# An encoder layer on one core: the operand builder adds before it splits, and the embedding tiles move to other steps and another engine

## Chip, cores and metric

One core of one Trainium2 chip. The metric is the device time of one execution in microseconds (us), the median of several runs; less is better. The engines are named as in the profile: PE (TensorE, the matmuls), DVE (VectorE), ACT (ScalarE), POOL (GpSimd) and SP (SyncE, which only issues transfers). A DMA is a transfer.

## What is computed

One layer of a bidirectional encoder, 512 tokens of width 1024, all in fp32:

```
h = h + 0.5 * swiglu(rms_norm(h, g_ffn1), w_ffn1_gate, w_ffn1_up, w_ffn1_down)      # hidden width 2816
u = rms_norm(h, g_mix) @ w_in
h = h + concat([mla(u), diff_attention(u)]) @ w_out                                 # 8 + 4 heads
h = h + 0.5 * swiglu(rms_norm(h, g_ffn2), w_ffn2_gate, w_ffn2_up, w_ffn2_down)
gate = sigmoid(rms_norm(h, g_ple_in) @ w_ple_gate + b_ple_gate)
h = h + gate * rms_norm(p @ w_ple_proj, g_ple_out)
```

## The kernel before

**Numbers in two parts.** An fp32 operand is split into a high part (a cast to `fp32r` by ACT) and a low part (what the cast left out, a subtraction on DVE). Each product is then three matmuls (`mm3`: high by high, high by low, low by high; L409 to L411). Weights come as 512 KB chunks by DMA, are split the same way (`Chunk`: cast L124, low part L97) and feed PE.

**The two feed-forward layers.** Each runs its 22 hidden blocks in four groups: one *plain* group of 4 blocks (gate and up projections, then the down projection to eight output tiles m = 0 to 7, named `ps_d`), then three groups of 6 blocks in which each pair of blocks takes two calls of `seven`. `seven` computes a 2 by 2 block product with seven smaller products in place of eight (Strassen-Winograd). In the order of the code these are S2 by T2, A11 by B11, S1 by N1, S3 by N3, A12 by B21, S4 by B22 and A22 by N4; three banks r1, r2, r3 hold them, ACT and DVE move them out to `q1`, `q2`, `q3` (L573 to L597). The weight side of a call is a `Unit`: two chunks `ra`, `rb` and a half chunk `rc`, sums formed partly by accumulating DMAs on POOL's queue (L157, L158) and partly by two POOL additions (L174, L175), then split into the tiles xa, xb, xc, xs. ACT casts xs in two halves (L187, L193).

**The builder.** The activation side is made once in each layer by `Forms.build`, for two halves (kp = 0, 1). It scales four tiles of h into a buffer y, splits the pieces used as they are (`sa`), forms four combinations n1, t2, n3, n4 on DVE, and splits these (`put`: a cast and a subtraction on a page named `fm`). It is a generator: `build(n)` runs n steps of it between other work of the plain group. Two of its splits, n3 and n4 of each half, are not done in it but put on the list `rest`; `finish_one`, called four times in the first `seven`, does one of them each time. The buffer y comes from a pool of three (`hlq`) that the units' tiles xa, xb, xs use too; y is free when the last of the four combinations has been read out of it.

**Order.** In the feed-forward layers PE, DVE, ACT and POOL run in the order of the code, each as a queue of its own: an instruction that waits holds up everything behind it on its engine. `slot(us)` and `steps(n)` decide where the splits of the next chunks stand, and `held` counts buffers. In the attention stage between the layers only PE keeps the order of the code; the other engines' order is chosen by a scheduler when the program is built.

**The embedding tiles.** `p @ w_ple_proj` is made in the attention stage by `embed`: after a first step that loads p, eight steps of six matmuls each into one bank (`ps_pe`), copied out by ACT (L1000) and sent to DRAM by POOL's queue (L1001). The attention stage runs over steps s_; in step s_ one block of scores of one head is computed, earlier heads' probabilities are transposed and multiplied, and `FILL_STEPS[s_]` says which other work ("T", "K", "E") is put in. "E" is one step of `embed`.

Of the kernel before, what the change touches and what calls it, by code (L numbers as in the profile page):

```python
# [18 lines left out]
TT = S // P  # L19
# [16 lines left out]

FILL_PRE = "TTTTTTTTTTTTTKTKTKTTT"
FILL_MID = "TKK"
FILL_STEPS = ("T", "TTE", "TT", "TT", "T", "") + ("E", "") * 6 + ("",) * 15 + ("E", "E")
HEADS = "DDMDMDMMMMMM"  # L40

GC = {"ffn1": 0, "mix": 8, "ffn2": 16, "ple_in": 24, "ple_out": 32, "b_ple": 40,
# [7 lines left out]
def encoder_layer(ctx, tc, xT, pT, wst, gcols, rows, consts, out):  # L50
    nc = tc.nc
# [368 lines left out]
    n1 = Norm("ffn1", nc.vector)  # L420
# [71 lines left out]
    class Forms:  # L492
# [11 lines left out]
        def build(self, kp):  # L504
            def v(t):
                return t.rearrange("p (a b) -> p a b", b=HS)

            def put(i, src):
                pg_ = page(f"fm{i}")
                d = pg_.rearrange("p x (a b) -> p x a b", b=HS)  # L510
                split(d[:, 0], d[:, 1], src)
                self.pg[kp][i] = pg_

            held[1] += 1
            y = hl_tile(1, "y", F32)
            ks = (2 * kp, 2 * kp + 1, 2 * kp + 4, 2 * kp + 5)
            for i, k in enumerate(ks):
                nc.vector.scalar_tensor_tensor(out=y[:, i // 2, (i % 2) * S:(i % 2 + 1) * S], in0=h[k],
                                               scalar=g(self.name, k), in1=self.rbc, op0=ALU.mult, op1=ALU.mult)
                yield  # L520
            q = [y[:, i].rearrange("p (a b) -> p a b", b=S) for i in range(2)]
            b11, b12 = q[0][:, :, :HS], q[0][:, :, HS:]
            b21, b22 = q[1][:, :, :HS], q[1][:, :, HS:]
            for i, k in enumerate(ks):

                c = slice(0, HS if i < 2 else S)
                a = self.sa[k] = page(f"sa{k}")
                split(a[:, 0, c], a[:, 1, c], y[:, i // 2, i % 2 * S:i % 2 * S + c.stop])
                yield
            n1, t2_, n3, n4 = [v(t2(f"f{i}")) for i in range(4)]  # L530
            nc.vector.tensor_sub(n1, b11, b12)
            put(self.N1, n1)
            yield
            nc.vector.tensor_add(t2_, b22, n1)
            put(self.T2, t2_)
            yield
            nc.vector.tensor_sub(n3, b12, b22)
            nc.vector.tensor_sub(n4, b21, t2_)
            held[1] -= 1
            self.rest.insert(kp, lambda: put(self.N3, n3))  # L540
            self.rest.append(lambda: put(self.N4, n4))
            yield

# [13 lines left out]
    def seven(forms, after=None):  # L557

        F_ = Forms
        A11, A12, S1, A22, S3, S2, S4 = nxt()  # L560
        r1, r2, r3 = psum("r1"), psum("r2"), psum("r3")
        q1, q2, q3 = t2("q1"), t2("q2"), t2("q3")
        lo, hi = slice(0, HS), slice(HS, S)

        def mul(r, left, i, start):
            x, c0 = left
            for k in range(4):
                c = slice(c0 + k * P, c0 + (k + 1) * P)
                bh, bl = forms.at(i, k)
                mm3(r[:, lo], x[:, 0, c], x[:, 1, c], bh, bl, start and k == 0, k == 3, skip_group_check=True)  # L570

        mul(r2, S2, F_.T2, True)
        nc.scalar.copy(q2[:, hi], r2[:, lo])  # L573
        forms.finish_one()
        steps(1)
        mul(r1, A11, F_.B11, True)
        nc.scalar.copy(q1[:, lo], r1[:, lo])
        forms.finish_one()
        steps(2)
        mul(r3, S1, F_.N1, True)  # L580
        nc.vector.tensor_add(q2[:, lo], r3[:, lo], q1[:, lo])
        forms.finish_one()
        steps(2)
        mul(r2, S3, F_.N3, False)
        nc.vector.tensor_sub(q3[:, hi], r2[:, lo], q2[:, lo])  # L585
        nc.vector.tensor_sub(q1[:, hi], q1[:, lo], q2[:, hi])
        forms.finish_one()
        steps(1)
        mul(r1, A12, F_.B21, False)
        after(0, r1[:, lo])  # L590
        steps(1)
        mul(r3, S4, F_.B22, False)
        nc.vector.tensor_add(q2[:, hi], r3[:, lo], q1[:, hi])
        after(1, q2[:, hi])
        steps(2)
        mul(r2, A22, F_.N4, False)
        nc.vector.tensor_sub(q3[:, lo], r2[:, lo], q1[:, lo])  # L597
        after(2, q3)
        steps(2)

    def ffn(norm, after, side=None, early=None):
# [39 lines left out]
        forms = builder = None  # L641
# [6 lines left out]
        for gi, (f0, n, plain) in enumerate(FGROUPS):  # L648
            hts = []
            if plain:  # L650
                late = []
                for f in range(n):
                    if f == 0 and early is not None:
                        psg, psu = early
                    else:
                        psg = psum("ps_g")
                        proj(psg, nxt(), norm.act)
                        slot(5.4)
                        if f == 1:
                            st_["r4"] = col_rsqrt(norm.acc, DM)  # L660
                        build(1)
                        psu = psum("ps_u")
                        proj(psu, nxt(), norm.act)
                        slot(3.5, f < n - 1)
                    late.append((psg, psu, hts))
                    if f == 1:
                        st_["rbc"] = row_bcast(st_["r4"])
                        forms = Forms(norm.name, st_["rbc"])
                        builder = (x for kp in range(2) for x in forms.build(kp))
                    if f > 0:  # L670
                        for e in late:
                            evac(*e)
                        late = []
                        build(3)
            else:
                build(99)
                for f in range(0, n, 2):
                    pair(hts)
            heads = []
            if plain:  # L680

                w = nxt()
                for m in range(3):
                    if m == 2:
                        while not ready:
                            advance()
                        w = ready[0].out
                    heads.append(psum("ps_d"))
                    proj(heads[m], w, hts, m % 2 * n, range(n - 1))
                    slot(1.3)  # L690
                    build(1)
                w = used[0].out
            for m in range(KT):
                if not plain:
                    ps = psum("ps_d")
                    proj(ps, nxt(), hts)
                else:
                    if m % 2 == 0 and m > 0:
                        w = nxt()
                    if m < 3:  # L700
                        ps = heads[m]
                        proj(ps, w, hts, m % 2 * n, range(n - 1, n))
                    else:
                        ps = psum("ps_d")
                        proj(ps, w, hts, m % 2 * n)
                if gi < len(FGROUPS) - 1 or m < KT - 1:
                    slot(0.0 if plain and m < 2 else 0.68 * n - (2.2 if gi == len(FGROUPS) - 1 else 0.75))
                if plain:
                    d = t2("hd")
                    nc.scalar.activation(d, ps, AF.Copy, scale=0.5)  # L710
                    nc.gpsimd.dma_start(out=h[m], in_=d, accum_op=ALU.add)
                else:
                    nc.vector.scalar_tensor_tensor(out=h[m], in0=ps, scalar=0.5, in1=h[m],
                                                   op0=ALU.mult, op1=ALU.add)
                last = gi == len(FGROUPS) - 1
                if last:
                    after(m)
                elif side is not None and (gi == 1 and m < KT // 2 + 1 or gi == 2 and m == 3):
                    for _ in range(2):
                        next(side, None)  # L720
                build(1 if m < 2 else 2)

    nmix = Norm("mix")
    h_dram = drp.tile([KT, P, S], F32, name="h_dram")
# [256 lines left out]
    def embed():  # L981
# [8 lines left out]
        for m in range(KT):  # L990
            if m % 4 == 0:
                w = chunk()
            ps = psum("ps_pe")
            for k in range(2):
                c = slice(((m % 4) * 2 + k) * P, ((m % 4) * 2 + k + 1) * P)
                mm3(ps, w[:, 0, c], w[:, 1, c], pa[k][0], pa[k][1], k == 0, k == 1)
            if m % 2 == 0:
                pg_ = page("pe", dt=F32)
            pe = pg_[:, m % 2, :]
            nc.scalar.copy(pe, ps)  # L1000
            nc.gpsimd.dma_start(out=pe_dram[m], in_=pe)  # L1001
            yield

# [425 lines left out]
```

## Time and profile before

| | us |
|---|---|
| median of 3 runs | 1046.29 (1044.59 to 1047.51) |
| the profiled execution, whole | 1045.17 |
| its span, first to last instruction | 1043.4 |
| PE busy (share of the span) | 1016.5 (97%) |
| DVE busy | 746.5 (72%) |
| ACT busy | 532.8 (51%) |
| POOL busy | 321.0 (31%) |
| PE share of the chain that ended last | 84% |

The first feed-forward layer stands at about 0 to 380 us, with its first `seven` at 78 us; attention and its projections to about 640 us; the second feed-forward layer after it, its first `seven` at 703 us; the last gate ends the program. In a timeline row the first number is the start in us from the span's start, the second the duration; in square brackets stands how long the engine had been idle before it and what ended that. The granted clock is a share of full speed (1.00 is 2.4 GHz, a half is 1.2 GHz).

### The profile page before, as it was taken

To read this page: it belongs to the slowest core of one execution; us is meant where nothing else is said; L and a number is where in the kernel's file an instruction comes from. 1 tells how busy PE (TensorE), PEld (TensorE's weight loads), DVE (VectorE), ACT (ScalarE), POOL (GpSimd) and SP (SyncE) were. 2 spreads that over 40 slices of the span, in tenths; PEclk is the share of its full clock that TensorE was granted. 3 is DMA by queue.
4 is the path that set the end of the run, shared out by engine and by line. 5 is a ranking of instruction groups with operands and counts; after the bars stand their busy time and mean duration, and the time that the engine had idled before them with its cause. 6 is when DMAs were issued, how large, how long until landed. Compare 5 with 4: busy or idle time off the path is not lost.

```text
span 1043.4 us, 16021 instructions
## 1 busy us (share of the span) xinstructions
PE 1016.5 (97%) x6076; PEld 893.1 (86%) x6076; DVE 746.5 (72%) x1258; ACT 532.8 (51%) x914; POOL 321.0 (31%) x291
## 2 busy tenths in 40 slices
PE   9988999999999999999999999988999999999998
PEld 7868998998999898876767888868998998999887
DVE  7786864875587648788788764686866875587764
ACT  7445532552354557478787643455534552354531
POOL 1144412532251210026553312044416532252000
PEclk9999999999999999999999999999999999999999
DMA  6367655656564542222103022367656655566331
GB/s 243 119 167 179 157 158 132 165 140 181 124 172 109 156 165 90 91 78 79 52 1 122 21 91 92 90 168 178 160 172 192 169 136 178 122 175 193 112 101 60
DMA packets 52621, 137.94 MB, mean 132 GB/s; under 512 B 6112, under 2 KB 7008, under 8 KB 52544
## 3 DMA queue, kind: packets, MB, share of 16 engines
q1 hardware_dynamic: 36864, 106.88, 30.9%
q0 software_dynamic: 14096, 27.66, 14.9%
q10 hardware_dynamic: 1584, 2.39, 0.6%
q8 instruction: 47, 0.77, 0.3%
q14 instruction: 30, 0.25, 0.1%
HBM read 126.02 MB, written 6.29 MB: 127 GB/s over the span
## 4 chain that ended last, share of the span: by engine, by line
PE 84%; DVE 9%; DMA 2%; issue 2%; ACT 2%; POOL 0%; SPq 0%; ACTq 0%; DVEq 0%; POOLq 0%
PE r L411 11%; PE r L410 11%; PE r L409 11%; PE ps_d L409 6%; PE ps_d L410 6%; PE ps_d L411 6%; PE ps_in L409 2%; PE ps_in L410 2%; PE ps_in L411 2%; PE ps_pt L1179 2%; PE ps_pg L409 1%; PE ps_pg L411 1%; PE ps_pg L410 1%; PE ps_wo L409 1%; PE ps_wo L411 1%
## 5 line engine op out<-in xcount | busy, mean ns | idle before, releaser
L97 DVE TENSOR_TENSOR hl<-raw,hl 128x1024 fp32r<-128x1024 f32 (+4 forms) x110 | 118.4, 1089 | 67.4 <-ACT hl L124 65.9
L124 ACT CAST hl<-raw 128x1024 fp32r<-128x1024 f32 (+2 forms) x104 | 96.3, 943 | 104.4 <-DMA raw<-in_wst_dram 30.5
L411 PE MATMUL ps_d<-ht,hl 128*128 128x512 f32 x352 | 137.3, 390 | 1.9 <-DVE hl L97 1.9
L409 PE MATMUL ps_d<-ht,hl 128*128 128x512 f32 x352 | 137.3, 390 | 0.0
L410 PE MATMUL ps_d<-ht,hl 128*128 128x512 f32 x352 | 137.1, 389 | 0.0
L174 POOL TENSOR_TENSOR ra<-ra,rb 128x512 f32<-128x512 f32 x36 | 49.6, 1378 | 219.2 <-DVE xa L97 214.3
L409 PE MATMUL r<-fm,xb 128*128 128x256 f32 x288 | 81.9, 284 | 4.5 <-DVE q L585 4.5
L409 PE MATMUL r<-sa,xa 128*128 128x256 f32 x288 | 82.3, 286 | 0.0
L410 PE MATMUL r<-sa,xa 128*128 128x256 f32 x288 | 82.3, 286 | 0.0
L411 PE MATMUL r<-sa,xa 128*128 128x256 f32 x288 | 82.2, 285 | 0.0
L410 PE MATMUL r<-fm,xb 128*128 128x256 f32 x288 | 81.6, 283 | 0.0
L411 PE MATMUL r<-fm,xb 128*128 128x256 f32 x288 | 81.5, 283 | 0.0
L411 PEld LDWEIGHTS ps_d<-ht,hl 128*128 128x128 f32 x352 | 66.1, 188 | 16.5 <-DVE hl L97 2.8
L409 PEld LDWEIGHTS ps_d<-ht,hl 128*128 128x128 f32 x352 | 66.1, 188 | 13.5
L410 PEld LDWEIGHTS ps_d<-ht,hl 128*128 128x128 f32 x352 | 66.1, 188 | 13.5
L175 POOL TENSOR_TENSOR ra<-ra 128x512 f32<-128x512 f32 x36 | 74.6, 2073 | 2.8
L157 POOL DMA_DIRECT2D rb<-in_wst_dram x36 | 32.4, 901 | 139.0 <-DMA rb<-in_wst_dram 92.1
L97 DVE TENSOR_TENSOR xa<-ra,xa 128x1024 fp32r<-128x1024 f32 x36 | 44.3, 1231 | 34.8 <-ACT xa L162 34.8
L97 DVE TENSOR_TENSOR xb<-rb,xb 128x1024 fp32r<-128x1024 f32 x36 | 65.0, 1805 | 0.4 <-ACT xb L166 0.4
L409 PEld LDWEIGHTS r<-fm,xb 128*128 128x128 f32 x288 | 55.4, 192 | 5.3 <-issue 3.8
L409 PEld LDWEIGHTS r<-sa,xa 128*128 128x128 f32 x288 | 56.1, 195 | 0.0
L410 PEld LDWEIGHTS r<-sa,xa 128*128 128x128 f32 x288 | 56.1, 195 | 0.0
(338 smaller groups left out, 3026.4 us busy)
## 6 DMA issues: line engine op xcount, KB each, us to landing
raw<-in_wst_dram SPq DMA_DIRECT2D x52, 512.0 KB, 3.5
rb<-in_wst_dram SPq DMA_DIRECT2D x36, 512.0 KB, 4.2
ra<-in_wst_dram SPq DMA_DIRECT2D x36, 512.0 KB, 3.6
raw<-in_wst_dram SPq DMA_DIRECT2D x48, 384.0 KB, 3.2
rc<-in_wst_dram SPq DMA_DIRECT2D x36, 256.0 KB, 4.3
rb<-in_wst_dram POOLq DMA_DIRECT2D x36, 256.0 KB, 4.9
rc<-in_wst_dram POOLq DMA_DIRECT2D x36, 256.0 KB, 6.2
h<-in_xT_dram SPq DMA_DIRECT2D x8, 256.0 KB, 5.0
```

The source lines that it names most:

```text
L97: nc.vector.tensor_sub(dst_l, src, dst_h.bitcast(F32))
L124: nc.scalar.copy(self.hl[:, 0, :self.n], self.raw[:, :self.n])
L157: nc.gpsimd.dma_start(out=self.rb[:, self.LO], in_=self.s1[:, self.HI], accum_op=ALU.add)
L174: nc.gpsimd.tensor_add(ra[:, LO], ra[:, LO], self.rb[:, LO])
L175: nc.gpsimd.tensor_add(ra[:, HI], ra[:, HI], ra[:, LO])
L409: MM(ps, lhsT=wh, rhs=ah, start=start, stop=False, **kw)
L410: MM(ps, lhsT=wh, rhs=al, start=False, stop=False, **kw)
L411: MM(ps, lhsT=wl, rhs=ah, start=False, stop=stop, **kw)
L1179: nc.tensor.transpose(out=ps[:, qt * P:(qt + 1) * P], in_=u.prs[qt][:, kt * P:(kt + 1) * P], identity=ident)
```

## The change

Three things. `build` forms all four combinations of a half first, in two steps, and then splits n1, t2 and n3 in three further steps; only the split of n4 stays on `rest`, so the first `seven` has two calls of `finish_one` in place of four. The builder has 13 steps for each half in place of 11, and more of them are run ahead: 2 for 1 between gate and up of a plain block, and 2 for 1 (m below 2) or 3 for 2 in the down projection. In the attention stage the eight "E" steps of tiles stand at s_ = 6, 8, 10, 14, 20, 22, 33, 34 (before: 6, 8, 10, 12, 14, 16, 33, 34), and the tile is copied out of its bank by DVE.

```diff
-FILL_STEPS = ("T", "TTE", "TT", "TT", "T", "") + ("E", "") * 6 + ("",) * 15 + ("E", "E")
+FILL_STEPS = ("T", "TTE", "TT", "TT", "T", "") + tuple("E" if s_ in (6, 8, 10, 14, 20, 22, 33, 34) else "" for s_ in range(6, 35))
...
             nc.vector.tensor_sub(n1, b11, b12)
-            put(self.N1, n1)
-            yield
             nc.vector.tensor_add(t2_, b22, n1)
-            put(self.T2, t2_)
             yield
             nc.vector.tensor_sub(n3, b12, b22)
             nc.vector.tensor_sub(n4, b21, t2_)
             held[1] -= 1
-            self.rest.insert(kp, lambda: put(self.N3, n3))
+            yield
+            put(self.N1, n1)
+            yield
+            put(self.T2, t2_)
+            yield
+            put(self.N3, n3)
             self.rest.append(lambda: put(self.N4, n4))
             yield
...
         mul(r2, S2, F_.T2, True)
         nc.scalar.copy(q2[:, hi], r2[:, lo])
-        forms.finish_one()
         steps(1)
         mul(r1, A11, F_.B11, True)
         nc.scalar.copy(q1[:, lo], r1[:, lo])
-        forms.finish_one()
         steps(2)
...
-                        build(1)
+                        build(2)
                         psu = psum("ps_u")
...
-                build(1 if m < 2 else 2)
+                build(2 if m < 2 else 3)
...
-            nc.scalar.copy(pe, ps)
+            nc.vector.tensor_copy(out=pe, in_=ps)
             nc.gpsimd.dma_start(out=pe_dram[m], in_=pe)
```

What this does to the order of instructions is shown at three places. The first is ACT at the end of the first layer's plain group, from the second half's last pieces to the first copies of the first `seven`; hd is the halved down projection of one m, fm the page of one split combination, f the combination. Before:

```order
L710 ACTIVATE hd<-ps_d 128x512
L93 CAST sa_633<-y 128x512
L93 CAST fm_641<-f_636 128x512
L710 ACTIVATE hd<-ps_d 128x512
L93 CAST fm_661<-f_637 128x512
L187 CAST xs<-ra 128x512
L193 CAST xs<-ra 128x512
L710 ACTIVATE hd<-ps_d 128x512 x3
L573 COPY q_730<-r_727 128x256
L93 CAST fm_745<-f_518 128x512
L162 CAST xa<-ra 128x1024
```

and now:

```order
L710 ACTIVATE hd<-ps_d 128x512
L93 CAST sa_620<-y 128x512
L187 CAST xs<-ra 128x512
L193 CAST xs<-ra 128x512
L710 ACTIVATE hd<-ps_d 128x512
L93 CAST fm_658<-f_623 128x512
L93 CAST fm_661<-f_624 128x512
L93 CAST fm_664<-f_625 128x512
L710 ACTIVATE hd<-ps_d 128x512 x4
L575 COPY q_736<-r_733 128x256
L162 CAST xa<-ra 128x1024
```

The casts of xs have moved ahead of the second half's split casts; three of these now stand in a row, four hd casts behind them, and none inside the first `seven` ahead of xa. The second place is DVE at the same point of the program; before:

```order
L531 TENSOR_TENSOR f_636<-y 128x512
L94 TENSOR_TENSOR fm_641<-f_636,fm_641 128x512
L534 TENSOR_TENSOR f_637<-y,f_636 128x512
L94 TENSOR_TENSOR fm_661<-f_637,fm_661 128x512
L537 TENSOR_TENSOR f_638<-y 128x512
L538 TENSOR_TENSOR f_639<-y,f_637 128x512
L97 TENSOR_TENSOR xs<-ra,xs 128x512 x2
L94 TENSOR_TENSOR fm_745<-f_518,fm_745 128x512
L94 TENSOR_TENSOR fm_763<-f_638,fm_763 128x512
L97 TENSOR_TENSOR xa<-ra,xa 128x1024
```

and now:

```order
L531 TENSOR_TENSOR f_623<-y 128x512
L532 TENSOR_TENSOR f_624<-y,f_623 128x512
L534 TENSOR_TENSOR f_625<-y 128x512
L535 TENSOR_TENSOR f_626<-y,f_624 128x512
L97 TENSOR_TENSOR xs<-ra,xs 128x512 x2
L94 TENSOR_TENSOR fm_658<-f_623,fm_658 128x512
L94 TENSOR_TENSOR fm_661<-f_624,fm_661 128x512
L94 TENSOR_TENSOR fm_664<-f_625,fm_664 128x512
L97 TENSOR_TENSOR xa<-ra,xa 128x1024
```

The four combinations stand together with no split between them, and fm_661, which is t2 of the second half, comes behind the two subtractions of xs. The third place is POOL at the same point, the accumulation of hd into h and the second unit's two accumulating transfers (one piece of the difference):

```order
 L175 TENSOR_TENSOR ra<-ra 128x512
 L711 DMA h_106<-hd 128x512 x2
-L711 DMA h_107<-hd 128x512 x2
-L711 DMA h_108<-hd 128x512
-L157 DMA rb<-in_wst_dram 128x512
-L158 DMA rc<-in_wst_dram 128x512
-L711 DMA h_108<-hd 128x512
+L711 DMA h_107<-hd 128x512
+L157 DMA rb<-in_wst_dram 128x512
+L158 DMA rc<-in_wst_dram 128x512
+L711 DMA h_107<-hd 128x512
+L711 DMA h_108<-hd 128x512 x2
```

The second unit's two transfers have moved ahead of two of the accumulations of hd. The same three places stand in the second feed-forward layer, with the same moves.

## Rows read from the trace of the kernel before

**Rows 1.** Stretches: start:end, length, busy us (instructions) by engine, clock, DMA, GB/s.

```profile
62.00:104.00 42.00, 35.35 (x223) 31.62 (x221) 31.57 (x41) 21.04 (x38) 22.48 (x20) 0.96 0.76 178
690.00:730.00 40.00, 32.92 (x212) 29.56 (x210) 29.64 (x40) 20.42 (x36) 21.76 (x20) 0.96 0.77 178
455.00:540.00 85.00, 82.32 (x436) 57.23 (x435) 68.90 (x176) 69.37 (x151) 45.84 (x52) 0.98 0.17 55
80.00:85.00 5.00, 5.00 (x33) 5.00 (x32) 1.69 (x3) 3.75 (x7) 1.83 (x3) 0.71 1.05 221
535.00:540.00 5.00, 5.00 (x24) 4.19 (x24) 3.71 (x10) 2.76 (x8) 1.73 (x3) 0.69 0.00 0
```

**Rows 2.** Waits of PE, whole span: total us, times, longest.

```profile
PE r L409 <- ACT xs L187: 5.4, 2, 2.7
PE r L409 <- DVE q L585: 4.5, 4, 1.7
...
PE ps_ss L365 <- ACT sqo L1157: 1.6, 1, 1.6
```

**Rows 3.** Timeline of PE, 62 to 109 us.

```profile
69.90 0.51 PE L411 MATMUL ps_d<-ht,hl 128*128 128x512 f32 x1 [0.98 <-DVE hl L97]
...
77.92 0.39 PE L409 MATMUL r<-fm,xs 128*128 128x256 f32 x1 [2.70 <-ACT xs L187]
...
82.86 0.30 PE L409 MATMUL r<-fm,xb 128*128 128x256 f32 x1
...
84.31 0.28 PE L409 MATMUL r<-fm,xc 128*128 128x256 f32 x1
...
90.52 0.36 PE L409 MATMUL r<-fm,xb 128*128 128x256 f32 x1 [1.73 <-DVE q L585]
...
105.53 0.39 PE L411 MATMUL r<-fm,xs 128*128 128x256 f32 x1 [1.48 <-DVE xs L97]
```

**Rows 4.** Timeline of ACT, 48 to 108 us.

```profile
77.25 0.62 ACT L187 CAST xs<-ra 128x512 fp32r<-128x512 f32 x1 [2.04 <-DVE f L538]
...
78.30 1.56 ACT L710 ACTIVATE hd<-ps_d 128x512 f32<-128x512 f32 x3
...
96.97 1.05 ACT L162 CAST xa<-ra 128x1024 fp32r<-128x1024 f32 x1 [2.16 <-DMA ra<-in_wst_dram]
```

**Rows 5.** Timeline of DVE, 48 to 108 us.

```profile
54.36 0.69 DVE L94 TENSOR_TENSOR ht<-v,ht 128x512 fp32r<-128x512 f32 x1 [0.69 <-ACT ht L93]
54.97 0.68 DVE L531 TENSOR_TENSOR f<-y 128x512 f32<-128x512 f32 x1
...
60.13 1.22 DVE L97 TENSOR_TENSOR hl<-raw,hl 128x1024 fp32r<-128x1024 f32 x1
...
64.86 3.51 DVE L518 SCALAR_TENSOR_TENSOR y<-h,gc,rbc 128x512 f32<-128x512 f32 x2
...
68.63 1.21 DVE L97 TENSOR_TENSOR hl<-raw,hl 128x1024 fp32r<-128x1024 f32 x1
...
76.46 0.68 DVE L538 TENSOR_TENSOR f<-y,f 128x512 f32<-128x512 f32 x1
...
87.74 2.31 DVE L97 TENSOR_TENSOR xb<-rb,xb 128x1024 fp32r<-128x1024 f32 x1
89.97 0.41 DVE L585 TENSOR_TENSOR q<-r,q 128x256 f32<-128x256 f32 x1
```

**Rows 6.** Timeline of POOL, 48 to 108 us.

```profile
66.19 1.63 POOL L175 TENSOR_TENSOR ra<-ra 128x512 f32<-128x512 f32 x1
```

**Rows 7.** Timeline of SP's DMA queue, 40 to 108 us.

```profile
90.18 0.33 SPq L154 DMA_DIRECT2D ra<-in_wst_dram  x1
```

**Rows 8.** DMA issues of 55 to 110 us: count, KB each, median us to landing.

```profile
h<-hd POOLq DMA_DIRECT2D x8, 256.0 KB, 7.0
```

**Rows 9.** The copies of the embedding tiles, by line: ns minimum, median, maximum.

```profile
L1000 ACT COPY pe<-ps_pe x8: 562/574/607, 481.4 to 558.1; 128x512 f32<-128x512 f32 x8
```

**Rows 10.** Groups of DVE by line, 455 to 540 us: total us, mean ns.

```profile
L1052 DVE TENSOR_REDUCE nmx<-ps_s 128x1 f32<-128x512 f32 x12 | 8.1, 676 | 0.7 <-PE ps_s L411 0.7
```

## The prediction

> **What bounds the kernel now.** I read the busy table first: PE works 97% of the span, so only what PE waits for, and the stretches in which its clock is low, can be won. The waits of PE give the places: the casts of xs (L187) twice 2.7 us, the copy of q at L585 four times, and one wait of 1.6 us in attention [rows 2]. The stretches then show how much that is. From 62 to 104 us PE is busy 35.35 of 42 us, from 690 to 730 us 32.92 of 40 [rows 1]: 6.65 and 7.08 us idle, around the first `seven` of either feed-forward layer. All waits are small elsewhere. From 80 to 85 us, after the 2.70 us wait, the granted clock is 0.71, a mix of both levels [rows 1]; at full clock a product of twelve matmuls takes 84.31 - 82.86 = 1.45 us [rows 3]. The low clock costs 0.29 x 5 = 1.45 us.
>
> In the timeline of PE the waits of the first layer stand in order [rows 3]: 0.98 us for a chunk's low part, 2.70 for xs, 1.73 for L585, and 1.48 at 105.53. The rows of ACT say what the xs cast at 77.25 waited for: the last combination, f L538 [rows 4], which ends at 76.46 + 0.68 = 77.14 [rows 5]. The cast does not read it. It needs the buffer that y holds, and y is read for the last time there. POOL had its input ready at 66.19 + 1.63 = 67.82 [rows 6].
>
> **The builder, first half.** DVE does the same instructions as before but no longer stands idle between a combination and its split. In a 0.69 us row the next starts 0.61 later (54.36 to 54.97 [rows 5]). Before, from the split of ht at 54.36 to the chunk's low part at 60.13 lie 5.77 us: ht, four combinations, two splits, and two idle gaps of about 0.69 like the one ahead of ht. Now the four combinations (2.4 us) go ahead of ht and push it from 54.36 to about 55.9 (part of them falls into idle time of DVE), then ht and three splits take 4 x 0.61 = 2.4: the low part starts at 58.4, 1.8 earlier. PE needs ht of the last block only in the down projection, after 58 us, so the push costs nothing; had it gone beyond, each us would be one of PE.
>
> **The builder, second half.** The two y rows at 64.86 (3.51 us together, [rows 5]) come 1.8 earlier and end at 66.6. Then three pieces of sa (0.34 + 0.34 + 0.6) stand ahead of the chunk's low part where one stood: it starts at 67.9, not 68.63, and PE's wait of 0.98 shrinks to 0.2. **Gain 0.8.** If the y rows don't move, the two added pieces make this wait 0.9 longer; that is the other bound.
>
> After the low part (1.14), xc and the last sa piece (1.2) come the four combinations (2.4): y is free at 72.7, 4.4 earlier than 77.14. ACT casts xs at 72.7 and 73.2, then hd, then n1 and t2 of the second half; the t2 cast ends at 75.4, its subtraction on DVE at 76.2. PE, 0.8 earlier than before, ends the down projection at 74.4 and finds xs ready, but its seventh and eighth matmul want t2 of the second half, which before was split ahead of xs. It waits until 76.2, about 1.1 us in place of 2.92 (2.70 and a following 0.22). **Gain 1.8.** Bounds: 2.9 if t2 is in time, 0 if the cast of t2 slips by 1.8.
>
> **The clock.** After the wait of 2.70 the clock fell; after those of 1.73 and 0.98 no stretch beside 80 to 85 is low. A wait of 1.1 should keep it. **Gain 1.45**, or 0.
>
> **The wait for L585.** What is queued on ACT from here: the cast of n3, four hd casts (three took 1.56 [rows 4]), the copy of r2 at 77.9, then xa. No split stands between them now; the two of n3 that stood inside the first `seven` are gone from there. xa is cast at 78.2, split by 80.4, xb split behind it in 2.31 us [rows 5] from about 82.2, L585 at 84.5 to 84.9. PE, six products of which the first ends at 76.8, is there at 76.8 + 5 x 1.45 = 84.05. It waits 0.9 to 1.4 in place of 1.73. **Gain 0.4**; bounds 0.8 and -0.5 (the five products at full clock, L585 a us later than reckoned).
>
> **What comes after.** The low part of xb frees the raw buffer for the next ra: xb ends at 90.05 [rows 5], ra is issued at 90.18 [rows 7] and cast at 96.97 [rows 4], 6.8 us on; the wait at 105.53 follows from it. With xb at 84.8 the same 6.8 us give 91.7, 5.2 earlier. POOL sends the second unit's two accumulating transfers ahead of two of hd now, after 68 us, so xb's data is no obstacle. So the later waits (about 2.5 us together) neither grow nor vanish, and the sum of the four gains, 0.8 + 1.8 + 1.45 + 0.4 = 4.45, is kept; the shift of ra would allow 5.2. I take 4.5. Its least is 1.0, if the DMA work, which hides behind nothing here (0.76 of all engines' time in the stretch [rows 1]), lets ra land only that much earlier; its most is all waits, 6.65, and the clock, 8.1. The second layer shows the same rows [rows 1, 2] and gets the same: **9.0 in all**, from 2 to 16.
>
> **The embedding tiles.** PE's matmuls are the same. ACT loses 8 x 0.574 = 4.6 us [rows 9]; DVE gains eight copies at about 0.676, the mean of another DVE instruction that reads 128 x 512 from a bank [rows 10], 5.4 us. Between 455 and 540 us DVE is busy 68.90 and ACT 69.37 of 85 us [rows 1]: neither covers for the other. What can be won is the wait of 1.6 us for sqo at 534 [rows 2] and the low clock behind it, 0.31 x 5 = 1.55 [rows 1]. Two tiles that stood at s_ = 12 and 16 now stand at 20 and 22, so up to s_ = 25 PE has the same work in sum, but the scores of s_ = 20 to 22, from which the chain to sqo starts, come up to 2.7 us earlier. Against that stand two copies on DVE in this very chain, 1.4. I take a gain of 2.0: the wait mostly gone, the clock kept, one us lost to waits of PE for a bank that DVE frees later. Bounds: +3.15 if all goes, and -4.1 if each of six copies in this stretch (6 x 0.676) holds up PE in full.
>
> The Trainium skill speaks against this part: "VectorE: DVE Perf Modes", section Specifications, says that VectorE sits closer to SBUF and ScalarE closer to PSUM. The rows agree, 676 ns against 574 [rows 9, 10]; by the rule alone the eight copies are an estimated 0.8 us of engine time dearer and the sum would be 0.8 worse, by the rows it is PE's waits that decide.
>
> **The sum.** 1045.17 - 9.0 - 2.0 = 1034.2 for the profiled execution. It stood 1.1 below the median of its runs, so I forecast 1046.29 - 11.0 = 1035.3.
>
> **Rivals.**
> - *The transfers hold the unit chain.* DVE and ACT come earlier, but ra of the third unit lands when the DMA work allows, 1.5 to 2 us earlier, and the gain moves into the waits of 1.73 and 1.48. For it: the DMA share of 1.05 from 80 to 85 us and 7.0 us to landing for each of the eight hd [rows 1, 8]. Against it: ra starts only when xb has been split. Each layer then gives 2: 1046.3 - 4 - 2 = 1040.3.
> - *Attention loses.* The copies queue on DVE ahead of the scores' chain: +4.1 in place of -2.0, hence 1046.3 - 9 + 4.1 = 1041.4.
> - *It doesn't do what it says.* Some other resource than y holds the xs cast and PE waits as before: 1046.3 - 2 = 1044.3. Against it: no other wait in the row of the cast.
> - *Slower: a new wait on ACT.* The buffer of q1 now follows that of an hd tile, and ACT, which works in order, stands at the copy of r1 until that hd has been accumulated; xb's cast, the last splits and the next unit stand behind it. hd of m = 3 is issued at about 74.4; with 7.0 us [rows 8] it lands at 81.4, 2.2 later than the copy could start, and the queue's slack takes up most of that. It decides from a landing of about 10 us on: at 13, each layer loses the 4.5, waits 1.5 more, and takes the low clock once: 1046.3 + 2 x 1.5 + 1.45 - 2 = 1048.8, and 1050.3 if both layers' clocks fall. For it: two transfers that now stand ahead of this hd on POOL.
>
> **How the numbers follow.** Forecast 0.66 (its own range 1031 to 1038.5); transfers 0.16; attention loses 0.09; nothing done 0.05; slower 0.04. A measurement of this kernel can tell about 0.3%, 3.1 us, from no change. Faster by more than that: 0.66 + 0.16 + 0.09 = 0.91; within it 0.06, the case of nothing done and the nearer half-case of the slower one; slower 0.03. The range of 8 in 10 holds the forecast, with the upper gains cut at 1030.5, and reaches to both middle rivals: 1030.5 to 1041.5.
>
> **What the profile after would show.** Right: the xs cast ends its wait at about 72.7, with the hd casts behind it; PE waits near 75 for t2's subtraction (fm, L94), about 1 us, in place of 2.70 for xs; granted clock 1.00 from 75 to 90; L585 near 84.7; ra's issue near 85; PE idle from 62 to 104 near 4 and not 6.65; no wait for sqo, and 1.00 at 530 to 540. Wrong: a clock below 0.9 after the new wait, ACT idle ahead of the copy of r1 for an hd transfer, an issue of ra later than 87, or new waits of PE for L1000.

## The result, and the profile after

The changed kernel takes 1032.66 us (median of 4 runs, 1031.20 to 1034.08); the kernel before took 1045.44 beside it. The ratio on record is 0.9882, with a 95% interval of 0.9866 to 0.9898: 12.3 us faster (12.8 between the two medians), where 11.0 (1035.3 us) was forecast. Run once more beside later experiments it gave 0.9879 [0.9866, 0.9893].

Where the time came from is read from three marks in PE's order: the first matmul of the first product behind the first feed-forward layer (ps_in), the last first-part matmul of the last product of attention (ps_wo), and the first one behind the second layer (ps_pg). The rows give, for one line and tile, the count, the shortest, median and longest duration in ns, and the start of the first and of the last in us. Before:

```profile
L409 PE MATMUL ps_in<-hl,act_mix x128: 347/389/501, 366.0 to 472.1; 128*128 128x512 f32 x96, 128*128 128x416 f32 x32
L409 PE MATMUL ps_wo<-oT,hl x32: 388/389/390, 610.6 to 631.7; 128*128 128x512 f32 x32
L409 PE MATMUL ps_pg<-act_ple_in,hl x72: 277/389/477, 993.1 to 1038.0; 128*128 128x512 f32 x56, 128*128 128x256 f32 x16
```

After:

```profile
L409 PE MATMUL ps_in<-hl,act_mix x128: 347/389/501, 362.3 to 468.4; 128*128 128x512 f32 x96, 128*128 128x416 f32 x32
L409 PE MATMUL ps_wo<-oT,hl x32: 388/390/390, 603.3 to 624.4; 128*128 128x512 f32 x32
L409 PE MATMUL ps_pg<-act_ple_in,hl x72: 278/390/478, 982.0 to 1026.9; 128*128 128x512 f32 x56, 128*128 128x256 f32 x16
```

The same marks were read in every run below; the numbers are differences of such rows, in us:

| run | up to ps_in: first layer | ps_in to ps_wo: attention | ps_wo to ps_pg: second layer |
|---|---|---|---|
| before | 366.0 | 265.7 | 361.4 |
| after | 362.3 | 262.1 | 357.6 |
| after, run again | 361.0 | 261.8 | 356.3 |
| e1, builder alone | 360.1 | 265.5 | 356.7 |
| e2, embedding alone | 365.9 | 262.5 | 359.9 |
| e3, its steps alone | 366.8 | 262.8 | 362.1 |
| e4, its copy alone | 364.9 | 266.5 | 361.0 |
| e5, old counts | 361.6 | 262.0 | 356.6 |
| e6, counts alone | 372.3 | 266.9 | 367.3 |
| e8, t2 first | 360.6 | 262.7 | 357.3 |
| e9, n4 early | 360.1 | 261.9 | 355.2 |
| e10, xb's low part later | 361.8 | 262.6 | 356.7 |
| e11, 14 filling products | 370.1 | 264.2 | 365.0 |
| e12, 9 filling products | 367.3 | 264.0 | 360.7 |

One execution differs from another by 1 to 2 us in a layer, so means are compared. The four runs with the builder of before (before, e2 to e4) average 365.9 and 361.1, the three with the new one (after twice, e1) 361.1 and 356.9: the builder gave 4.8 and 4.2, **9.0 together, the number that was forecast**. That it fits so closely is chance: taken one by one against the same means, the three executions gave 7.1, 9.7 and 10.2. For attention, before, e1, e6, e11 and e12 average 265.3, and the eight runs with the new steps 262.3: 3.0, where 2.0 was forecast. (e4, with the old steps and the new copy, is left out; with it the first mean is 265.5.)

The stretches of after, to be read against [rows 1] (the later ones are shifted by the time already won): start:end, length, busy us by engine (PE, PEld, DVE, ACT, POOL), clock, DMA share, GB/s.

```profile
62.00:104.00 42.00, 36.82 (x244) 32.92 (x242) 32.07 (x46) 21.57 (x40) 22.07 (x20) 1.00 0.81 188
682.00:722.00 40.00, 34.62 (x232) 30.97 (x231) 29.07 (x43) 20.69 (x38) 20.75 (x20) 1.00 0.83 189
...
80.00:85.00 5.00, 5.00 (x44) 5.00 (x43) 3.30 (x4) 3.39 (x8) 4.74 (x6) 1.00 1.13 204
531.00:536.00 5.00, 5.00 (x28) 3.93 (x28) 4.50 (x14) 4.63 (x12) 2.64 (x4) 1.00 0.00 0
```

The clock is 1.00 everywhere. In 80 to 85 us PE starts 44 matmuls, and 33 before [rows 1]. PE is idle for 5.18 us from 62 to 104, where near 4 was forecast: the wait of 1.48 at the third unit, behind 104 in the kernel before, now lies inside. PE's waits in the first layer, with the row that was the 2.70 us wait (75.01, no wait now), and one row of the second layer:

```profile
69.90 0.50 PE L411 MATMUL ps_d<-ht,hl 128*128 128x512 f32 x1 [0.41 <-DVE hl L97]
75.01 0.28 PE L409 MATMUL r<-fm,xs 128*128 128x256 f32 x1
76.41 0.38 PE L409 MATMUL r<-fm,xs 128*128 128x256 f32 x1 [0.52 <-ACT fm L93]
77.22 0.39 PE L410 MATMUL r<-fm,xs 128*128 128x256 f32 x1 [0.43 <-DVE fm L94]
86.22 0.35 PE L409 MATMUL r<-fm,xb 128*128 128x256 f32 x1 [0.96 <-DVE q L585]
101.87 0.39 PE L411 MATMUL r<-fm,xs 128*128 128x256 f32 x1 [1.48 <-DVE xs L97]
...
701.44 0.39 PE L409 MATMUL r<-sa,xa 128*128 128x256 f32 x1 [1.10 <-ACT q L578]
```

Four waits stand where the prediction put them: hl shorter, xs gone, t2 (fm) in its place, L585 shorter. The wait of 1.48 at the third unit came along unchanged, from 105.53 [rows 3] to 101.87. The last row is new: PE waits for the copy of r1. ACT tells why; its first two rows are the xs cast and the three splits, the others the copy of r1 in the first and second layer:

```profile
73.69 0.62 ACT L187 CAST xs<-ra 128x512 fp32r<-128x512 f32 x1 [3.80 <-DVE f L535]
75.23 1.65 ACT L93 CAST fm<-f 128x512 fp32r<-128x512 f32 x3
81.48 0.37 ACT L578 COPY q<-r 128x256 f32<-128x256 f32 x1 [1.44 <-DMA h<-hd]
...
701.01 0.37 ACT L578 COPY q<-r 128x256 f32<-128x256 f32 x1 [3.03 <-DMA hb<-hd]
```

The xs cast still waits for the last combination, which now ends at 72.90 + 0.69 = 73.59 on DVE in place of 77.14, and ACT does stand for the accumulation of hd, which the prediction lists as a sign of being wrong. DVE:

```profile
72.90 0.69 DVE L535 TENSOR_TENSOR f<-y,f 128x512 f32<-128x512 f32 x1
```

The chain of work that ended last runs in the first layer, from the xs cast on, through hd and its accumulating transfer to SP's queue and the next ra (start, duration; then what SP waited for between 60 and 110 us):

```profile
78.73 6.97 DMA h<-hd
85.77 0.33 SPq L150
86.27 7.01 DMA ra<-in_wst_dram
```

```profile
SPq L150 <- DMA h<-hd: 9.7, 1, 9.7
```

L150 loads rc of a later unit into a buffer that an hd held, and ra (L154) stands behind it in SP's queue. That transfer landed at 85.70, and the split of xb, which frees the buffer for ra, ended at 84.53 + 1.21 = 85.74: had one been faster, the other would still have held ra. In the second layer the chain runs through an hd as well (7.37 us), there by way of the copy of r1.

In these two runs of the changed kernel, what the first layer gains is how much earlier its third unit gets its weights. The wait of 1.48 there came 105.53 - 101.87 = 3.66 us earlier and the first layer ended 366.0 - 362.3 = 3.7 earlier; in the second run that row stands at 100.50, 5.03 earlier, and the layer ended 5.0 earlier. In both runs ra was issued at 86.3 to 86.4; its transfer took 7.0 us in one and 5.5 in the other, and that makes the 1.3 us between them.

In attention the wait of PE for sqo, the squares of one head's output, has nearly gone (total, times, longest):

```profile
PE ps_ss L365 <- ACT sqo L1157: 0.3, 1, 0.3
```

### The profile page after: what moved, and what is told of

The parts are those of the page before. It is cut to its first block, busy times and chain, and to the rows that moved or that the text cites. A ratio compares the mean times of both kernels' runs of the same rounds, so it can differ in the third digit from the quotient of the medians.

```text
span 1032.3 us, 16024 instructions
## 1 busy us (share of the span) xinstructions
PE 1011.9 (98%) x6076; PEld 889.1 (86%) x6076; DVE 747.1 (72%) x1266; ACT 528.0 (51%) x906; POOL 320.0 (31%) x291
## 4 chain that ended last, share of the span: by engine, by line
PE 79%; DVE 9%; DMA 6%; issue 3%; ACT 2%; POOL 1%; SPq 0%; ACTq 0%; DVEq 0%; POOLq 0%
PE r L411 9%; PE r L409 9%; PE r L410 9%; PE ps_d L409 6%; PE ps_d L411 6%; PE ps_d L410 6%; PE ps_in L409 3%; PE ps_in L411 2%; PE ps_in L410 2%; PE ps_pt L1179 2%; PE ps_pg L409 1%; PE ps_pg L410 1%; PE ps_wo L409 1%; PE ps_pg L411 1%; PE ps_wo L411 1%
## 5 line engine op out<-in xcount | busy, mean ns | idle before, releaser
L175 POOL TENSOR_TENSOR ra<-ra 128x512 f32<-128x512 f32 x36 | 74.5, 2069 | 2.8
```

The costliest lines, as they stand in the source:

```text
L175: nc.gpsimd.tensor_add(ra[:, HI], ra[:, HI], ra[:, LO])
```

## The experiments

**e1 to e4: the parts by themselves.** e1 takes the embedding part back:

```diff
-FILL_STEPS = (... "E" if s_ in (6, 8, 10, 14, 20, 22, 33, 34) ...)
+FILL_STEPS = (... ("E", "") * 6 + ("",) * 15 + ("E", "E"))
...
-            nc.vector.tensor_copy(out=pe, in_=ps)
+            nc.scalar.copy(pe, ps)
```

> The builder's part alone (order of combinations and splits, number of steps run ahead); the embedding tiles as in the kernel before. Theory: the two parts add up, and the first matmul of the stage behind either feed-forward layer shows what this one brings, 366.0 - 362.3 = 3.7 us in the first and 11.1 - 7.3 = 3.8 in the second: 7.5 us, ratio 0.9928. The waits of PE for xs of 2.70 us are gone, the clock from 75 to 85 us is 1.00, a wait of about 1.0 us for t2 of the second half stands in their place. Rival, the later layers gain because the stages before them end earlier: the whole 11 us would be here, ratio 0.989, or under 5 us, above 0.995.

Measured: 0.9909 [0.9894, 0.9924], 9.5 us. The 7.5 read from one profile of after was low, and outside the interval; the 9.0 of the prediction lies inside the interval. The parts add up, and attention (265.5) shows nothing of the builder.

e2 puts the embedding part alone into the kernel before (both edits above the other way round):

> The embedding part alone (steps 14, 20, 22 in place of 12, 14, 16, and the copy on VectorE); the builder as before. Theory: 3.6 us, which is 7.3 - 3.7 at the last matmul of the stage: ratio 0.9966. The wait of 1.60 us for sqo and the low clock of 535 to 540 us are gone. The prediction took 2.0, ratio 0.998. Rival: under 1 us, and the 3.6 were the chance of the scheduler's order behind the new builder.

Measured: 0.9972 [0.9960, 0.9984], 2.9 us. e3 has the new steps with the copy left on ACT, e4 the copy on DVE at the old steps:

> The moved steps alone, the copy of the tiles on ScalarE as before. Theory (the moved steps bring scores of s_ = 20 to 22 earlier, and the chain to sqo starts from these): most of the gain of the embedding part, 2.5 to 3.6 us, ratio 0.9966 to 0.9976, and no wait for sqo above 0.5 us. Rival (ScalarE, relieved of 4.6 us of copies, makes sqo in time): under 1 us, the wait for sqo stays near 1.6 and the clock behind it falls.

> The copy on VectorE alone, the tiles at the steps of before. Theory (the steps matter): within 1 us of before, ratio 0.999 to 1.001, the wait for sqo stays above 1 us. Rival (the engine matters): 2.5 to 3.6 us faster, ratio 0.9966 to 0.9976. Third case (the copies of 0.68 us hold the score chain on VectorE): slower by up to 4.1 us, ratio 1.004, with new waits of PE in the stretch of 480 to 530 us.

Measured: e3 0.9976 [0.9965, 0.9987], e4 1.0000 [0.9986, 1.0013]. **The steps make the gain; which engine copies makes no measurable difference.** The wait of PE for sqo in e3 and then e4, and e4's stretch behind that wait:

```profile
PE ps_ss L365 <- ACT sqo L1157: 0.7, 1, 0.7
```

```profile
PE ps_ss L365 <- ACT sqo L1157: 1.7, 1, 1.7
```

```profile
535.00:540.00 5.00, 5.00 (x16) 4.01 (x17) 2.56 (x8) 1.63 (x4) 1.01 (x2) 0.50 0.00 0
```

At the old steps the wait stays and the clock is at its lower level (1.2 GHz) for the five us behind it; at the new steps the wait is 0.7 and the clock 1.00. But the wait alone does not decide the clock: in e1, e11 and e12, also with the old steps, PE waited the same 1.60 and the stretch behind it stayed at 1.00; the row is e11's, where that wait ended at 538.63:

```profile
540.00:545.00 5.00, 5.00 (x29) 3.79 (x28) 3.82 (x12) 3.96 (x10) 2.48 (x5) 1.00 0.01 3
```

The times of the stage go with the clock: e11 and e12, where no stretch of 440 to 570 us is below 1.00, took 264.2 and 264.0 us; before, e4 and e6, with a low stretch behind that wait, 265.7, 266.5 and 266.9, and e1, with one at 470 (0.68), 265.5. Against e11 and e12 the new steps (262.3) still won 1.8.

**e5 and e6: order or number of steps.** e5 is the changed kernel with the old numbers, e6 the kernel before with the new numbers:

```diff
 (e5; e6 has the reverse, in the kernel before)
-                        build(2)
+                        build(1)
...
-                build(2 if m < 2 else 3)
+                build(1 if m < 2 else 2)
```

> The changed kernel with the old number of steps run ahead (build(1) in the plain blocks; 1 for m below 2 and 2 after that). Theory (what counts is when the last combination has read y): by counting steps the combinations of the second half end in the second half's tenth step, the 23rd of 26; with the old numbers that is behind m = 5 of the down projection, before the change (22nd of 22) behind m = 4, in the changed kernel behind m = 2. So the wait of PE for xs is at least as long as before, 2.7 us or up to 5, the low clock returns, and the gain of the builder is gone: ratio 0.995 to 1.005 with the embedding part's 0.997 in it. Rival (the new order of combinations and splits by itself frees y early): ratio 0.988 to 0.992 as in the changed kernel.

Measured: 0.9870 [0.9847, 0.9893]. The theory was wrong, the rival right: the order alone brings the whole gain of the builder. DVE and PE in e5:

```profile
72.26 0.68 DVE L531 TENSOR_TENSOR f<-y 128x512 f32<-128x512 f32 x1
...
74.18 0.68 DVE L535 TENSOR_TENSOR f<-y,f 128x512 f32<-128x512 f32 x1
```

```profile
75.65 0.39 PE L409 MATMUL r<-fm,xs 128*128 128x256 f32 x1 [1.12 <-ACT xs L187]
77.90 0.39 PE L410 MATMUL r<-fm,xs 128*128 128x256 f32 x1 [0.34 <-DVE fm L94]
```

The four combinations start no earlier than in the kernel before (72.26 here, 71.91 in the trace of before) but take 2.6 us, to 74.86, and not 5.2 to 77.14: between them lay two subtractions and two stretches of DVE waiting for a cast. The two in the kernel before:

```profile
73.27 0.69 DVE L94 TENSOR_TENSOR fm<-f,fm 128x512 fp32r<-128x512 f32 x1 [0.69 <-ACT fm L93]
75.25 0.69 DVE L94 TENSOR_TENSOR fm<-f,fm 128x512 fp32r<-128x512 f32 x1 [0.69 <-ACT fm L93]
```

Counting generator steps against m, as I did, says little: what decides is when DVE gets to them. The larger numbers of the change trade these waits for that of hl (0.41, none in e5) and gain nothing over it.

> The kernel before with the new number of steps run ahead alone (2 for 1, 3 for 2), combinations and splits in the old order, embedding as before. Theory (order and numbers both matter): the combinations now end behind m = 2, but two splits with their idle gaps stand between them, about 2 us; y is free near 75.5 to 76 and not at 73.6, PE waits 1.5 to 2 us for xs in place of 2.92, and nothing for t2, which is split ahead of it. 2 to 5 us faster (the upper end if the clock stays at 1.00), ratio 0.995 to 0.998. Rival (the numbers alone do it): 9 us, ratio 0.991. Second rival (the order alone does it): no gain, ratio 0.999 to 1.001.

Measured: 1.0112 [1.0087, 1.0136], **11.7 us slower**: none of the three cases. ACT, then PE:

```profile
86.56 0.60 ACT L710 ACTIVATE hd<-ps_d 128x512 f32<-128x512 f32 x1 [5.82 <-DMA h<-hd]
```

```profile
88.93 0.58 PE L409 MATMUL r<-fm,xc 128*128 128x256 f32 x1 [5.03 <-ACT fm L93]
```

This is the slower rival of the prediction in kind, at another instruction: not at the copy of r1 but at a later hd, ACT, in order, stands 5.82 us for a buffer whose accumulation has not landed (median to landing here 7.4), and the split that PE needs stands behind it. It is not the whole loss: ahead of it PE waited 1.04 and 1.58 us for hl, where the kernel before has 0.98, and the clock falls (0.83 between 70 and 80 us, 0.70 and 0.62 in the two stretches from 85 to 95). How the 11.7 divides is not shown.

**e8 and e9: the two waits that are new.** e8 splits t2 ahead of n1; e9 also splits n4 of the first half behind the combinations of the second:

```diff
             held[1] -= 1
+            self.finish_one()      # e9 alone
             yield
-            put(self.N1, n1)
-            yield
             put(self.T2, t2_)
             yield
+            put(self.N1, n1)
+            yield
```

> The changed kernel with t2 split ahead of n1 in either half, since the first product of the first seven wants t2 and n1 only the third. Theory (the new wait of 0.95 us, 0.52 for the cast and 0.43 for the subtraction of t2 of the second half, is the place of t2 in the queue of three splits): cast and subtraction come 0.52 and 0.6 us earlier, the two waits shrink to 0.0 to 0.4 us, about 0.6 us a layer are won and part of it is given to the next wait: 1035.3 to 1031 us in the measure of this text, ratio 0.9865 to 0.988. Rival (the wait passes on to L585 or to the copy of q at L578): the same as the changed kernel, 0.988, with the waits for t2 gone and those at L578 and L585 longer by as much.

Measured: 0.9879 [0.9860, 0.9899], the same as the changed kernel. Its waits:

```profile
76.33 0.39 PE L410 MATMUL r<-fm,xs 128*128 128x256 f32 x1 [0.34 <-DVE fm L94]
82.56 0.38 PE L409 MATMUL r<-sa,xa 128*128 128x256 f32 x1 [1.07 <-ACT q L578]
```

The wait for t2 fell from 0.95 to 0.34, as in the theory; what it won went into the wait for the copy of r1, which stands for hd. That is the rival.

> As e8_t2first, and n4 of the first half is split right behind the combinations of the second half, where ACT stands idle for 3.8 us and DVE for 0.76, in place of between the copy of r1 and L585. That also shifts the buffers: q1 now takes the buffer of the third combination, and ACT no longer stands at the copy of r1 for the accumulation of hd of m = 3 (1.44 us in the first layer). Theory: the waits of PE at L578 (1.10 in the second layer) and L585 (0.96 and 0.62) shrink to under 0.5 each, 1 to 1.5 us a layer more than e8: ratio 0.984 to 0.986. Rival (xb of the second unit, or the third unit's ra, lands no earlier, and PE waits there): as e8, 0.9865 to 0.988.

Measured: 0.9861 [0.9838, 0.9884], 1030.69 us. The wait for the copy of r1 is gone in both layers, since q1 no longer follows an hd; one of 1.20 for L586 (the former L585) is left in its place:

```profile
85.46 0.39 PE L409 MATMUL r<-fm,xb 128*128 128x256 f32 x1 [1.20 <-DVE q L586]
```

It is the lowest median of all, but its interval overlaps that of the changed kernel; that it is better is not shown.

**e10: the last wait of the place.** On top of e9, in the first `seven` the subtraction for xb goes behind the copy:

```diff
+        first = bool(forms.rest)
         forms.finish_one()
-        steps(2)
+        steps(0 if first else 2)
...
-        steps(1)
+        steps(3 if first else 1)
```

> As e9_n4early, and in the first seven of a layer the subtraction for xb (2.3 us while POOL adds, 1.2 else) stands on DVE behind the copy of r2 to q3 and not ahead of it. Theory (the last wait of the place, 1.20 us in either layer, is this one subtraction in front of the copy): the copy starts near 82.5 in place of 85.0, PE's wait for it is gone, and the second unit's later waits stay under 0.5 us: 1.0 to 1.2 us a layer, 2.0 to 2.4 in all, ratio 0.982 to 0.985. Rival (xb, and with it the next ra, comes about 1 us later and PE waits in the second or third unit): as e9, 0.985 to 0.987, with a wait for xs or xa of about 1 us behind it.

Measured: 0.9890 [0.9875, 0.9905]: the mechanism is the rival's, the time a little above the 0.985 to 0.987 that it named. The wait of 1.20 is gone, and PE waits for xs and then, 0.86 us, in the third unit for a copy on ACT:

```profile
87.46 0.38 PE L411 MATMUL r<-fm,xs 128*128 128x256 f32 x1 [1.05 <-DVE xs L97]
```

```profile
81.88 1.42 DVE L94 TENSOR_TENSOR fm<-f,fm 128x512 fp32r<-128x512 f32 x1 [0.18 <-ACT fm L93]
...
83.56 1.18 DVE L588 TENSOR_TENSOR q<-q,q 128x256 f32<-128x256 f32 x1
```

```profile
81.46 1.29 POOL L174 TENSOR_TENSOR ra<-ra,rb 128x512 f32<-128x512 f32 x1 [0.19 <-DVE xa L97]
```

POOL's second addition (L175) follows from 82.83 to 84.46. A subtraction on DVE with both inputs in SBUF takes longer while POOL adds: this one 1.42 us and not 0.69, the small one 1.18 and not 0.41; now that xb's subtraction, 2.31 us in e9, is moved out of the way (it takes 1.2), others pay. One that reads a bank does not: L581 took 0.42 us in the changed kernel, at 81.88, beside POOL's addition of 81.39 to 82.69. The Trainium skill ("SBUF — State Buffer", Who interferes with whom) says that a DVE instruction with two SBUF inputs contends with a GpSimd instruction that reads SBUF; these rows agree.

> The changed kernel itself once more, beside e10 and e11 on one chip: ratio 0.986 to 0.990. Its profile shows how much one execution differs from another: the same waits in the two feed-forward layers within 0.3 us (xs none, t2 0.5 + 0.4, L585 0.6 to 1.0, L578 up to 1.1), and the clock at 1.00.

Measured: 0.9879 [0.9866, 0.9893]. hl 0.42, t2 0.52 + 0.43 and L585 0.95 repeat to 0.01 us in the first layer. In the second, ACT stood 1.17 for hd and not 3.03, and PE did not wait for the copy of r1: that wait differs between executions of one program.

**e11 and e12: the clock by itself.** Products of constants fill PE's wait for xs in the kernel before, 14 in e11, 9 in e12:

```diff
+        if forms.rest:
+            for _ in range(14):
+                MM(r2[:, :P], lhsT=ident, rhs=ident, start=True, stop=True)
         mul(r2, S2, F_.T2, True)
```

> The kernel before, with 14 products of constants (128x128 each, into the bank that the first product of seven then overwrites) put on PE where it waits 2.70 us for xs; nothing else is changed, and these add nothing to the result. They take about 0.13 us each, 1.8 to 2.0 us, and so fit into the wait. Theory (the stall costs twice, once as a wait and once by the low clock behind it): the wait for xs is 0.6 to 1.0 us in the profile, the clock from 80 to 85 us is 1.00, and 1.45 us a layer come back: 2.9 us faster, ratio 0.9972, bounds 0.996 to 0.9985. Rival (what follows waits for L585 anyway, and the low clock is hidden in that wait): within 0.5 us of before, ratio 0.9995 to 1.0005, with the wait for L585 longer by what the clock gave. Second rival: the products of constants overrun the wait and it is slower, ratio above 1.0005.

Measured: 1.0078 [1.0066, 1.0091], slower, and hardly for the reason of the second rival. The products took 3.29 us, more than the wait of 2.70, yet PE started on `seven` 0.79 us behind the start of the xs cast, where it was 0.67 before. The rows behind are these, PE and ACT:

```profile
88.15 0.56 PE L409 MATMUL r<-fm,xc 128*128 128x256 f32 x1 [3.80 <-ACT fm L93]
```

```profile
87.20 0.37 ACT L580 COPY q<-r 128x256 f32<-128x256 f32 x1 [4.53 <-DMA h<-hd]
```

Buffers are handed out when the program is built. With 14 more matmuls on PE, q1 got the buffer of hd of m = 5, and ACT stood 4.53 us for it. No instruction of ACT had changed, and with 9 (e12) the same copy did not wait.

> The kernel before with 9 products of constants in the wait for xs in place of the 14 of e11_busy. There each took 0.235 us (3.29 for 14), so 9 take 2.1 us and end inside the wait of 2.70; and with 9 the buffer of q1 is the one it has in the kernel before, which with 14 it was not. The products add nothing to the result. Theory (the low clock costs on its own): the wait for xs is about 0.6 us, the clock from 80 to 85 us is 1.00, and what the prediction took for the clock comes back, 1.45 us a layer, 2.9 in all: ratio 0.9972, bounds 0.996 to 0.9985. Rival (PE only arrives earlier at the next wait, for L585): ratio 0.9995 to 1.0005, and the wait for L585 grows from 1.73 to about 3.0 us. Between: L585 itself comes earlier by what its chain takes from PE, and about half comes back, 0.9985 to 0.9995.

Measured: 1.0002 [0.9986, 1.0018]. PE in both layers, then two stretches of the first:

```profile
79.39 0.39 PE L409 MATMUL r<-fm,xs 128*128 128x256 f32 x1 [0.74 <-ACT xs L187]
90.84 0.36 PE L409 MATMUL r<-fm,xb 128*128 128x256 f32 x1 [2.04 <-DVE q L588]
...
703.02 0.39 PE L409 MATMUL r<-fm,xs 128*128 128x256 f32 x1 [0.74 <-ACT xs L187]
714.45 0.35 PE L409 MATMUL r<-fm,xb 128*128 128x256 f32 x1 [2.02 <-DVE q L588]
```

```profile
80.00:85.00 5.00, 4.88 (x40) 4.88 (x41) 2.03 (x5) 4.67 (x9) 2.65 (x3) 1.00 1.06 219
90.00:95.00 5.00, 4.08 (x22) 3.81 (x23) 4.19 (x9) 1.65 (x4) 1.01 (x2) 0.72 0.85 145
```

The clock stays at 1.00 from 80 to 85, and from the row that waits for xs to the row that waits for L585 PE needs 11.45 and 11.43 us in place of 90.52 - 77.92 = 12.60 and 12.58: 1.15 a layer, with the next wait 0.3 longer. In the whole time nothing of the 2.3 is seen; the interval allows 1.5 at most. In the first layer the clock falls behind the longer wait instead (0.72 from 90 to 95), and this program came to the place 1.5 us later, for which no row here gives a reason (e2, with the same builder, came as late). The third unit shows where the 1.15 goes: from the row that waits for hl to its wait of 1.47 PE needs 106.83 - 71.36 = 35.47 and 730.06 - 694.99 = 35.07 us, before 35.63 and 35.53. Of 1.15 a layer 0.16 and 0.46 are left, since ra lands hardly earlier. So in the feed-forward layers the local price of the clock is shown; by itself it is worth 0.6 us in these two profiles, too little for the measured times to tell from nothing.

## Why the prediction was right, point by point

- **First half, hl: 0.8 forecast, 0.57 measured** (0.98 to 0.41; 0.97 to 0.41 in the second layer). The two y rows end at 67.4 and not at 66.6. e11 and e12, which keep the old builder, have 0.95 to 0.97; the runs with the new order and numbers have 0.35 to 0.5.
- **Second half, xs and t2: 1.8 forecast, 1.97 measured** (2.70 + 0.22 to 0.52 + 0.43). y was free at 73.6 and not 72.7, t2 late as predicted. The mechanism, a buffer and not data, is shown by e5: the release moves from 77.14 to 74.86, the xs cast follows it, and PE with that. A fourth buffer, which would test the buffer alone, wasn't tried.
- **Clock: 1.45 forecast, about 1.56 in the first layer and 1.04 in the second.** From its arrival at the hl wait to the end of that for L585 PE needed 90.52 - 68.92 = 21.60 us before and 86.22 - 69.49 = 16.73 now: 4.87 (forecast 4.45). The waits explain 0.57 + 1.97 + 0.77; the rest, 1.56, is put down to the clock. In the second layer the same two marks lie 21.57 and 18.05 us apart: 3.52, of which the waits explain 0.56 + 1.92 + 1.10 - 1.10 (the new wait for the copy of r1) and leave 1.04. e12 shows 1.15 directly. But the prediction adds this to what the layer gains, and e12 says that it does not go there by itself. What moved the layer's end is the earlier ra, which hangs on y, xs and the splits behind them.
- **L585: 0.4 forecast, 0.77 measured** (1.73 to 0.96) in the first layer, at 86.2 and not at 84.7, since ACT came to xb later, having stood 1.44 us for hd at the copy of r1.
- **What comes after: as forecast.** ra is issued at 86.27 (90.18 before), and the three waits behind, 0.44, 0.64 and 1.48, are near the 0.45, 0.57 and 1.48 of before, with 0.30 for a copy of r1 added. ra's cast came 96.97 - 93.31 = 3.66 us earlier in this profile, 5.05 in the run again, where 5.2 was allowed and 4.5 taken.
- **Transfers hold the chain:** not as this rival had it; its 2 us a layer did not come. ra's cast comes 7.0 us behind its issue, 6.8 before [rows 4, 7]. But its argument against, that ra starts only when xb has been split, is only half of it: in the first layer ra's issue also stood behind an hd's transfer, which landed 0.04 us before that split ended.
- **The slower rival** was real, at the size the text gave for its near end: ACT stood 1.44 and 3.03 us for hd (the first copy of r1 started at 81.48, the landing was forecast at 81.4), PE 1.10 in one of the four places that the two profiles of the changed kernel hold. e6 and e11 show the far end: 5.82 and 4.53 us of ACT, 11.7 and 8.1 us slower. It deserved more than 0.04: that the change escaped its far end hangs on which hd's buffer q1 was given.
- **Attention: 2.0 forecast, 3.0 measured** (2.9 by e2's time). This is the term that was mis-sized, and by what was left out. The forecast was 1.6 for sqo and 1.55 for the clock, less one us for PE waiting for a bank that DVE frees later. sqo gave 1.34 (1.60 to 0.26). The banks cost 0.69: a wait of 0.27 (ps_trd, for the copied tile) and one of 0.59, where ACT's copy had made PE wait 0.17 at the same matmul:

```profile
478.85 0.47 PE L409 MATMUL ps_s<-kT,mq 96*128 96x512 f32 x1 [0.59 <-DVE dmx L1126]
```

Not counted were a wait of 0.60 for DVE (pt), which went, and 0.15 of low clock in the next stretch (0.97 from 540 to 545). Together 1.34 + 1.55 + 0.15 + 0.60 - 0.69 = 2.95. The copies took 682 ns, 5.5 us in all, and e4 shows that they cost nothing that can be measured. The Trainium skill ("VectorE: DVE Perf Modes", Specifications) says that VectorE sits closer to SBUF and ScalarE closer to PSUM; the trace agrees as far as the times go, 682 ns against 574, and here it does not decide. The copies of after, ns shortest, median and longest, against [rows 9]:

```profile
L1000 DVE COPY pe<-ps_pe x8: 666/682/692, 482.6 to 551.7; 128x512 f32<-128x512 f32 x8
```

## What to carry to other kernels

A wait that names an operand can be a wait for its buffer: look for the last reader of what held it before, and put the reads together, ahead of work that goes back and forth between two engines. Behind an engine that works in order, ask of every tile that it writes who had the buffer, and whether a transfer still reads it: here kernels in which it went badly were 8 to 12 us slower (e11, e6), and in e11 it changed with an edit on another engine. That holds for the queue that issues transfers too. And the last wait of a place is followed by the next: of three edits that took one away (e8 to e10), none was measurably faster.

## What was not expected of the hardware

The clock does not follow one wait's length. In e5's second layer it fell to its lower level behind three short waits (PE's timeline, and the stretch behind it):

```profile
691.83 0.39 PE L409 MATMUL r<-fm,xs 128*128 128x256 f32 x1 [0.56 <-ACT xs L187]
692.56 0.39 PE L411 MATMUL r<-fm,xs 128*128 128x256 f32 x1 [0.23 <-DVE xs L97]
694.11 0.58 PE L409 MATMUL r<-fm,xs 128*128 128x256 f32 x1 [0.82 <-ACT fm L93]
```

```profile
695.00:700.00 5.00, 5.00 (x24) 5.00 (x25) 1.61 (x2) 2.53 (x5) 1.93 (x2) 0.50 1.08 271
```

In e5's first layer waits of 1.12, 0.22 and 0.34 left it at 1.00. The low stretch cost that second layer nothing that shows: it took 356.6 us, the changed kernel 357.6 and 356.3. In e12 it fell behind one of 2.04 in the first layer (0.72) and not behind one of 2.02 in the second (1.00 from 690 to 730). In e4's first layer, with the builder of before, a wait of 2.75 for xs left it at 1.00 from 75 to 90, and it fell behind the next one, of 2.04 (0.66 from 90 to 95). The prediction's step from "a wait of 1.1" to "keeps the clock" came out right, but these rows would not have carried it as a rule.
